# Fixing TensorE's order to that of the source in the pairs of a feed-forward block

## The chip, the cores and the metric

The kernel runs on one core of one Trainium2 chip. The metric is the device time of one execution in microseconds (us); lower is better. The core's engines run side by side, each with an instruction order of its own that is fixed when the program is compiled: TensorE (PE: matrix products; its weight loads are listed as PEld), VectorE (DVE), ScalarE (ACT), GpSimd (POOL) and SyncE (SP), which here issues almost all DMAs. An engine waits on semaphores for the others' results.

## The reference

Two layers of a decoder act on 256 tokens of width 2048, in float32. Of one layer:

```python
h = rms_norm(x, pre_mix_gain[i])
m = hybrid_mixer(h, ..., w_in[i], ..., w_out[i])    # attention and a gated recurrence
x = x + rms_norm(m, post_mix_gain[i])
h = rms_norm(x, pre_ffn_gain[i])
f = (silu(h @ w_ffn_gate[i]) * (h @ w_ffn_up[i])) @ w_ffn_down[i]    # 2048 -> 5632 -> 2048
x = x + rms_norm(f, post_ffn_gain[i])
gate = sigmoid(rms_norm(x, ple_gain[i]) @ w_ple_gate[i])
x = x + (p[i] @ w_ple_proj[i]) * gate
```

What matters here is the line of `f`: the gate, up and down products, with weights of 2048x5632, 2048x5632 and 5632x2048.

## The kernel before

**Precision.** Every float32 product is made of three products of the reduced type fp32r. A weight block of 128x1024 (two row blocks of 128, 512 columns) is fetched raw (`wr`, 10 buffers), ScalarE casts its high part (`wh`, 7 buffers, L305), VectorE subtracts to get the low part (`wl`, 7 buffers, L315), and activations have a high and a low part too. For each row block TensorE then issues high x high (L419), low x high (L422) and high x low (L423); a block thus takes six products, each 128x128 by 128x512. The order of the three is in `acc`, L415.

**Strips and pairs.** A strip computes one set of 512 output columns for both halves of the tokens (t = 0, 1). A pair (`paired`, L400) computes two sets of columns at once, into four PSUM banks. In a pair, a group of two blocks of rows, two sets of columns and two token halves is multiplied by the scheme of Strassen and Winograd: seven block products in place of eight, from sums of activations (`mixed`, `mixed_turned`) and differences of raw weights that VectorE makes in place (L435). The bank `u` carries product 1, is copied to SBUF by ScalarE (`saved`, L428), goes on with product 5 (`second`, L469), is copied again, goes on with product 7 (`third`, L473) and is copied once more; then it serves as the fourth output bank. The rest of the rows goes through `plain` (L483) as ordinary blocks, the first set of columns with the banks `acce` and `acca`, then the second set with `accc` and `u` (which is `ms` in the trace, as it comes from the pool of L107).

In source order a pair issues: products 1 (`u`), 2 (`accc`), 3 (`acce`), 4 (`acca`); the first plain block (`acce`, `acca`); product 5 (`u`); the further plain blocks of the first columns; product 6 (`accc`) and 7 (`u`); the plain blocks of the second columns. With `mixed_order` the last two plain blocks of both sets of columns come at the very end.

**The pairs of a layer.** The output projection has two pairs (L1144). The feed-forward block has ten pairs of a gate and an up column set (n = 1 to 10, `gated`, L1156; n = 0 goes as two strips), each with two sets of seven products (`more`), so 84 products in `fast` and 96 in `plain`. Between them stand the down products, in four groups of 2, 3, 3 and 3 column sets of hidden activations: each group makes a pair of output columns (0, 1) and a pair (2, 3), but the last group does (2, 3) as strips: seven down pairs, each with one set of seven. The per-layer gate at the end has one pair (L1283), with `after`.

**From the hidden block to the down pair.** `done_up` multiplies gate and up, transposes within blocks on VectorE (L251), stores to DRAM and fetches back in another order (`shuffled`, L241; SyncE issues both), and `split_shuffled` (L279) makes the high part on ScalarE (L203) and the low part on VectorE (L204). So the last hidden block of a group is still under way when the first down pair of that group starts. The transposed block, the fetched block, `saved` copies and gate values share the 12 buffers of the tag `nat` (L59).

**The order of the work.** The kernel is written against a scheduler that runs when the program is compiled. For each engine it takes, of the instructions whose inputs and buffers its own time model says are ready, the one that is earliest in the source; a later one may overtake an earlier one that it holds not to be ready. That order is then fixed; on the chip an engine takes its instructions strictly in it. `behind(...)` (L80) puts the instructions of a block, on the engine of a marked instruction, after that instruction.

Of the kernel before, what the change touches and what calls it, by code (L numbers as in the profile page):

```python
# [26 lines left out]
SKEW = 5  # L27
# [20 lines left out]
def decoder(ctx: ExitStack, tc: tile.TileContext, x, p, positions, w_in, attn_sinks,  # L48
# [16 lines left out]
    V, S, G, T = nc.vector, nc.scalar, nc.gpsimd, nc.tensor  # L65
# [13 lines left out]
    @contextmanager  # L79
    def behind(*names):  # L80

        with ExitStack() as st:
            for n in names:
                st.enter_context(tc.issue_after(marks[n].ins))
            yield
# [9 lines left out]
    def tick():  # L95
        clock[0] += 1
        for gen in list(running):
            if next(gen, True):
                running.remove(gen)
        for item in [q for q in queue if q[0] <= clock[0]]:  # L100
            queue.remove(item)
            item[1]()

    def nat(shape=(P, W), dt=F32):
        return np_.tile(list(shape), dt, tag="nat", name="nat")

    def bank(shape=(P, W)):  # L107
        return pms.tile(list(shape), F32, tag="ms", name="ms")
# [88 lines left out]
    def square_sum(src, acc, shape=(P, W)):  # L197
        j = np_.tile([P, W], F32, tag="junk", name="junk", bufs=1)
        S.activation(j[:, 0:shape[1]], src, AF.Square, accum_out=acc)
# [97 lines left out]
    def fetch_w(w, c, col):  # L297
        raw = wpr.tile([P, 2, W], F32, tag="wr", name="wr")
        nc.sync.dma_start(raw, w[c * 2 * P:(c + 1) * 2 * P, col:col + W].rearrange(
            "(k p) n -> p k n", p=P))  # L300
        return raw
# [6 lines left out]
    def load_w(w, c, col, raw=None, hi=None):  # L308

        if raw is None:  # L310
            raw = fetch_w(w, c, col)
        if hi is None:
            hi = high(raw)
        lo = wps.tile([P, 2, W], F32R, tag="wl", name="wl")
        marks["lo"] = V.tensor_tensor(lo, raw, hi.bitcast(F32), op=ALU.subtract)  # L315
        return hi, lo
# [81 lines left out]
        return both  # L398

    def paired(lhs, sums, wa, wb, cols, done_a, done_b, nch=8, row0=0, skews=(0, 0),  # L400
               after=None, mixed_order=False, more=None, q=0):

        base = row0 // (2 * P)
        opened = {}

        def psum(name):
            return pacc.tile([P, W], F32, tag="acc", name=name)

        def block(c, t):
            def get(k):  # L410
                kt = 2 * c + k
                return tuple(a[:, kt % 4, t * P:(t + 1) * P] for a in lhs[kt // 4])
            return get

        def acc(ps, x, hl, ks=(0, 1)):  # L415
            hi, lo = hl
            for k in ks:
                xh, xl = x(k)
                T.matmul(ps, xh, hi[:, k], start=id(ps) not in opened, stop=False,  # L419
                         skip_group_check=True)  # L420
                opened[id(ps)] = ps
                T.matmul(ps, xl, hi[:, k], start=False, stop=False, skip_group_check=True)  # L422
                marks["pe"] = T.matmul(ps, xh, lo[:, k], start=False, stop=k == ks[-1],  # L423
                                       skip_group_check=True)

        def saved(ps):
            b = nat()
            S.copy(b, ps)  # L428
            return b

        def parts(r):
            return load_w(None, 0, 0, raw=r)

        def sub(dst, p, q):
            V.tensor_tensor(dst, p, q, op=ALU.subtract)  # L435

        def fast():
            quads = [(sums(), q)] + ([(more(), q + 2)] if more else [])
            raw = [[fetch_w(w, base + c, col) for w, col in zip((wa, wb), cols)] for _, c in quads]
            for r, (_, c) in zip(raw, quads):  # L440
                r += [fetch_w(w, base + c + 1, col) for w, col in zip((wa, wb), cols)]

            def each(fn):
                for (mix, c), r in zip(quads, raw):
                    fn(mix, c, *r)
            u = psum("accu") if after else bank()
            each(lambda mix, c, r11, r12, r21, r22: acc(u, block(c, 0), parts(r11)))
            x = [saved(u)]
            each(lambda mix, c, r11, r12, r21, r22: sub(r11, r12, r11))
            cc = psum("accc")  # L450
            each(lambda mix, c, r11, r12, r21, r22: acc(cc, mix(1), parts(r11)))
            p5 = saved(cc)
            tick()
            e = psum("acce")
            each(lambda mix, c, r11, r12, r21, r22: acc(e, block(c + 1, 0), parts(r21)))
            if more:
                tick()

            def fourth(mix, c, r11, r12, r21, r22):
                sub(r11, r22, r11)  # L460
                sub(r21, r21, r11)
            each(fourth)
            a = psum("acca")
            each(lambda mix, c, r11, r12, r21, r22: acc(a, block(c + 1, 1), parts(r21)))
            tick()
            each(lambda mix, c, r11, r12, r21, r22: sub(r12, r22, r12))
            y = []

            def second():  # L469
                each(lambda mix, c, r11, r12, r21, r22: acc(u, mix(2), parts(r11)))  # L470
                y.append(saved(u))

            def third():  # L473
                each(lambda mix, c, r11, r12, r21, r22: acc(cc, mix(4), parts(r22)))
                each(lambda mix, c, r11, r12, r21, r22: acc(u, mix(3), parts(r12)))
                x.append(saved(u))
                y.append(p5)
                tick()
            return e, a, cc, u, x, y, second, third

        rest = [i for i in range(nch) if not q <= i < q + (4 if more else 2)]

        def plain(w, col, banks, skew, end, cs=rest, then=None):  # L483
            n = len(cs)
            ws = {}
            for i in range(n + skew):
                if i < n:
                    ws[i] = load_w(w, base + cs[i], col)
                    acc(banks[0], block(cs[i], 0), ws[i])
                    if i == n - 1 and end:  # L490
                        end(0)
                if i >= skew:
                    acc(banks[1], block(cs[i - skew], 1), ws[i - skew])
                if then and i == 0:
                    then()
                tick()
            if end:
                end(1)

        e, a, c, d, x1, x2, second, third = fast()  # L500

        def end_a(t):
            done_a(t, (e, a)[t], x1[t])

        def end_b(t):
            done_b(t, (c, d)[t], x2[t])
        if mixed_order:
            plain(wa, cols[0], (e, a), 0, None, cs=rest[:-2], then=second)
            third()
            plain(wb, cols[1], (c, d), 0, None, cs=rest[:-2])  # L510
            plain(wa, cols[0], (e, a), 0, end_a, cs=rest[-2:])
            plain(wb, cols[1], (c, d), 0, end_b, cs=rest[-2:])
            return
        def then():
            second()
            if after:
                after[0]()
        plain(wa, cols[0], (e, a), skews[0], lambda t: t or end_a(t), then=then)
        third()
        end_a(1)  # L520
        if after:
            after[1]()
        plain(wb, cols[1], (c, d), skews[1], end_b)

    def load_gain(g, col):
        b = np_.tile([P, W], F32, tag="gB", name="gB", bufs=2)
        nc.sync.dma_start(b, g[col:col + W].partition_broadcast(P))
        return b
# [199 lines left out]
    for l in range(DEPTH):  # L728
# [403 lines left out]
        def merged(s):  # L1132
            gB = load_gain(post_mix_gain[l], s * W)

            def done(t, ps):
                if t == 0:
                    mg.append(sp.tile([P, NT, W], F32, tag="ABCD"[s], name=f"mg{s}"))
                square_sum(ps, ssm[t][:, s:s + 1])
                V.tensor_tensor(mg[s][:, t], ps, gB, op=ALU.mult)
                if s == 3:  # L1140
                    post_norm(mg, ssm, t, ss, xT, gain_cols(32, l, 16), 4)
            return summed(done)
        for s in (0, 2):
            paired(mixT, lambda: sums, w_out[l], w_out[l], (s * W, s * W + W), merged(s),  # L1144
                   merged(s + 1), skews=(0, SKEW if s == 2 else 0))


        rx2 = lazy_rstd(ss, "ry")
# [41 lines left out]
        for gi, glen in enumerate(FF_GROUPS):  # L1190
# [11 lines left out]
            for s in range(4):  # L1202
# [31 lines left out]
                elif s % 2:  # L1234
                    paired(hid, lambda: hx[0], w_ffn_down[l], w_ffn_down[l], (s * W - W, s * W),
                           dones[s - 1], done, nch=2 * glen, row0=ff0 * W,
                           mixed_order=s == 1 and glen > 2, q=2)
# [37 lines left out]
        for s in (0, 1):  # L1275
# [3 lines left out]
            if s == 0:  # L1279
# [5 lines left out]
               after=(lambda: projected(2, pa), lambda: projected(3, pb)))  # L1285
# [32 lines left out]
```

## Time and profile before

| | |
|---|---|
| time, median of 3 runs (lowest to highest) | 2384.71 us (2380.53 to 2385.95) |
| the profiled execution, its own time | 2386.15 us |
| its span, first to last instruction | 2384.4 us |
| PE busy | 2351.7 us (99%), 10891 products |
| DVE busy | 2072.3 us (87%) |
| ACT busy | 1421.3 us (60%) |
| granted TensorE clock, mean | 0.997 |
| feed-forward pairs, first layer | 439.3 to 1060.3 us |
| feed-forward pairs, second layer | 1623.4 to 2244.1 us |

A row of the timeline gives the start, the length, the engine, the source line, the operation and `out<-in` by the program's names, and in brackets the engine's idle time before it with what ended it. A product has a length of some 0.39 us from its start to its modelled end, but products overlap in the array. A row of the windows gives, for a stretch, its length, and for each engine the busy time with the number of instructions, then the granted TensorE clock (1.00 is full), the share of the DMA engines' time and GB/s.

### The profile page before, as it was taken

The numbers are of one execution on the slowest core, as the hardware profiler recorded it, in microseconds if no ns is written. First come the engines' busy times: TensorE is split into PE (matmuls) and PEld (weight loads), VectorE is DVE, ScalarE is ACT, GpSimd is POOL, SyncE is SP. The second block draws the span as 40 slices with busy tenths as digits, with TensorE's granted clock in tenths as the row PEclk, the third lists the DMA queues.
The fourth block names the chain that finished last, engine by engine and source line by source line (L and its number), as shares of the span: only waits on it lengthen the run. The fifth ranks groups of instructions, "written<-read, shape, count | busy, mean of one in ns | idle before, by whom it ended". The sixth has DMA issues, their size and how long they took to land.

```text
span 2384.4 us, 31615 instructions
## 1 busy us (share of the span) xinstructions
PE 2351.7 (99%) x10891; PEld 1939.8 (81%) x10891; DVE 2072.3 (87%) x2671; ACT 1421.3 (60%) x2022; POOL 104.2 (4%) x213
## 2 busy tenths in 40 slices
PE   9999999999999999999999999999999999999999
PEld 7888887887888878888788888878777888888887
DVE  7687977999999999987877879779999999999885
ACT  6565466666656655656656554575666566566564
POOL 3100001000000000001010000010000000000010
PEclk9999999999999999999999999999999999999999
DMA  8666467666565764775766563774766576657853
GB/s 289 216 187 202 150 202 246 213 211 229 186 222 205 254 230 155 257 256 192 240 217 213 180 211 131 230 250 172 243 212 204 185 251 212 225 190 248 276 165 133
DMA packets 301666, 506.03 MB, mean 212 GB/s; under 512 B 23713, under 2 KB 69697, under 8 KB 301505
## 3 DMA queue, kind: packets, MB, share of 16 engines
q1 hardware_dynamic: 301200, 503.93, 63.2%
q8 instruction: 85, 1.39, 0.2%
q14 instruction: 77, 0.62, 0.1%
q0 software_dynamic: 64, 0.02, 0.0%
q10 hardware_dynamic: 240, 0.07, 0.0%
HBM read 474.57 MB, written 29.36 MB: 211 GB/s over the span
## 4 chain that ended last, share of the span: by engine, by line
PE 82%; DVE 11%; issue 3%; DMA 2%; ACT 1%; POOL 1%; SPq 0%; DVEq 0%; ACTq 0%; POOLq 0%
PE acc L330 9%; PE acc L331 9%; PE acc L333 9%; PE ms L419 5%; PE ms L423 5%; PE ms L422 5%; PE accc L423 4%; PE accc L422 4%; PE accc L419 4%; PE acca L423 4%; PE acca L419 4%; PE acca L422 4%; DVE wl L315 3%; PE acce L423 3%; PE acce L419 3%; PE acce L422 3%
## 5 line engine op out<-in xcount | busy, mean ns | idle before, releaser
L305 ACT CAST wh<-wr 128x1024 fp32r<-128x1024 f32 x1020 | 1039.0, 1052 | 699.6 <-DVE wr L435 222.2
L315 DVE TENSOR_TENSOR wl<-wr,wh 128x1024 fp32r<-128x1024 f32 x1020 | 1209.7, 1220 | 178.5 <-ACT wh L305 174.1
L330 PE MATMUL acc<-wh,ck 128*128 128x512 f32 x1056 | 418.0, 396 | 0.7 <-ACT ck L203 0.7
L331 PE MATMUL acc<-wh,ck 128*128 128x512 f32 x1056 | 413.2, 392 | 0.0
L333 PE MATMUL acc<-wl,ck 128*128 128x512 f32 x1056 | 411.8, 391 | 0.8 <-DVE wl L315 0.8
L435 DVE TENSOR_TENSOR wr<-wr 128x1024 f32<-128x1024 f32 x240 | 285.4, 1217 | 1.1
L333 PEld LDWEIGHTS acc<-wl,ck 128*128 128x128 f32 x1056 | 198.4, 188 | 42.8 <-DVE wl L315 1.7
L330 PEld LDWEIGHTS acc<-wh,ck 128*128 128x128 f32 x1056 | 198.8, 188 | 40.7 <-ACT ck L203 1.0
L331 PEld LDWEIGHTS acc<-wh,ck 128*128 128x128 f32 x1056 | 199.0, 188 | 39.9 <-DVE ck L204 0.2
L423 PE MATMUL acca<-wl,ck 128*128 128x512 f32 x448 | 177.3, 396 | 6.0 <-DVE wl L315 5.8
L419 PE MATMUL acca<-wh,ck 128*128 128x512 f32 x448 | 176.2, 393 | 2.3 <-ACT wh L305 1.6
L422 PE MATMUL acce<-wh,ck 128*128 128x512 f32 x448 | 175.0, 391 | 2.9 <-DVE ck L204 2.7
L419 PE MATMUL acce<-wh,ck 128*128 128x512 f32 x448 | 174.9, 390 | 2.7 <-ACT wh L305 2.7
L422 PE MATMUL acca<-wh,ck 128*128 128x512 f32 x448 | 175.6, 392 | 0.0
L423 PE MATMUL acce<-wl,ck 128*128 128x512 f32 x448 | 174.4, 389 | 0.0
L419 PE MATMUL ms<-wh,ck 128*128 128x512 f32 x420 | 164.7, 392 | 2.1 <-ACT nat L428 2.1
L422 PE MATMUL ms<-wh,ck 128*128 128x512 f32 x420 | 163.5, 389 | 0.0
L423 PE MATMUL ms<-wl,ck 128*128 128x512 f32 x420 | 163.2, 389 | 0.0
L422 PE MATMUL accc<-wh,ck 128*128 128x512 f32 x328 | 127.6, 389 | 0.0
L423 PE MATMUL accc<-wl,ck 128*128 128x512 f32 x328 | 127.6, 389 | 0.0
L419 PE MATMUL accc<-wh,ck 128*128 128x512 f32 x328 | 127.6, 389 | 0.0
L423 PEld LDWEIGHTS acca<-wl,ck 128*128 128x128 f32 x448 | 84.8, 189 | 29.5 <-DVE wl L315 11.5
(281 smaller groups left out, 3302.9 us busy)
## 6 DMA issues: line engine op xcount, KB each, us to landing
wr<-in_w_in_dram SPq DMA_DIRECT2D x176, 512.0 KB, 4.8
wr<-in_w_ffn_gate_dram SPq DMA_DIRECT2D x176, 512.0 KB, 5.5
wr<-in_w_ffn_up_dram SPq DMA_DIRECT2D x176, 512.0 KB, 6.2
wr<-in_w_ffn_down_dram SPq DMA_DIRECT2D x176, 512.0 KB, 7.1
wr<-in_w_out_dram SPq DMA_DIRECT2D x64, 512.0 KB, 4.8
wr<-in_w_ple_gate_dram SPq DMA_DIRECT2D x64, 512.0 KB, 5.3
turn<-nat SPq DMA_DIRECT2D x86, 256.0 KB, 2.1
nat<-turn SPq DMA_DIRECT2D x344, 64.0 KB, 3.4
```

Source lines behind the costliest of these rows:

```text
L305: marks["hi"] = S.copy(hi, raw)
L315: marks["lo"] = V.tensor_tensor(lo, raw, hi.bitcast(F32), op=ALU.subtract)
L330: T.matmul(ps[t], xh, hi[:, k], start=first, stop=False)
L331: T.matmul(ps[t], xl, hi[:, k], start=False, stop=False)
L333: marks[t, c] = marks["pe"] = T.matmul(ps[t], xh, lo[:, k], start=False, stop=last)
L419: T.matmul(ps, xh, hi[:, k], start=id(ps) not in opened, stop=False, skip_group_check=True)
L422: T.matmul(ps, xl, hi[:, k], start=False, stop=False, skip_group_check=True)
L423: marks["pe"] = T.matmul(ps, xh, lo[:, k], start=False, stop=k == ks[-1], skip_group_check=True)
L435: V.tensor_tensor(dst, p, q, op=ALU.subtract)
```

## The change

All TensorE instructions that `paired` issues are put under a manual schedule of that one engine, so that TensorE keeps the order of the source within a pair. The products of `fast` (1 to 4, and what it defines) are moreover put behind the last product issued before in the source (`behind("pe")`), so that a pair does not start before the one ahead of it has ended. Pairs with `after` (the per-layer gate) and pairs called with the new argument `free=True` (the output projection) keep the scheduler's order. So the 10 gate and up pairs and the 7 down pairs of each layer are concerned. The body of `paired` moves into an inner function `products`, with nothing else changed. No instruction is added or removed on any engine, no tile, buffer or DMA changes.

```diff
     def paired(lhs, sums, wa, wb, cols, done_a, done_b, nch=8, row0=0, skews=(0, 0),
-               after=None, mixed_order=False, more=None, q=0):
+               after=None, mixed_order=False, more=None, q=0, free=False):
...
-        e, a, c, d, x1, x2, second, third = fast()
+
+        def products(pin):
+            with behind("pe") if pin else nullcontext():
+                e, a, c, d, x1, x2, second, third = fast()
...
+            if mixed_order:
+                plain(wa, cols[0], (e, a), 0, None, cs=rest[:-2], then=second)
+                third()
+                plain(wb, cols[1], (c, d), 0, None, cs=rest[:-2])
+                plain(wa, cols[0], (e, a), 0, end_a, cs=rest[-2:])
+                plain(wb, cols[1], (c, d), 0, end_b, cs=rest[-2:])
+                return
...
+            plain(wa, cols[0], (e, a), skews[0], lambda t: t or end_a(t), then=then)
             third()
...
+            plain(wb, cols[1], (c, d), skews[1], end_b)
+
+        pin = not (after or free)
+        with tc.manual_schedule(engines={T.engine}) if pin else nullcontext():
+            products(pin)
...
             paired(mixT, lambda: sums, w_out[l], w_out[l], (s * W, s * W + W), merged(s),
-                   merged(s + 1), skews=(0, SKEW if s == 2 else 0))
+                   merged(s + 1), skews=(0, SKEW if s == 2 else 0), free=True)
```

More of the change, by code (lines that the diff above doesn't have):

```diff
@@ L498, in plain, with end_a, end_b, then @@
                 end(1)
-        e, a, c, d, x1, x2, second, third = fast()
[L502 to L508, printed above, removed]
-            third()
[L510 to L515, printed above, removed]
-            if after:
[L517 to L523, printed above, removed]
+        def products(pin):
+            with behind("pe") if pin else nullcontext():
+                e, a, c, d, x1, x2, second, third = fast()
+            def end_a(t):
+                done_a(t, (e, a)[t], x1[t])
+            def end_b(t):
+                done_b(t, (c, d)[t], x2[t])
+            if mixed_order:
[5 more added lines that the diff above has]
+                return
+            def then():
+                second()
+                if after:
+                    after[0]()
+            plain(wa, cols[0], (e, a), skews[0], lambda t: t or end_a(t), then=then)
+            third()
+            end_a(1)
+            if after:
+                after[1]()
+            plain(wb, cols[1], (c, d), skews[1], end_b)
+        pin = not (after or free)
+        with tc.manual_schedule(engines={T.engine}) if pin else nullcontext():
+            products(pin)
     def load_gain(g, col):
```

## The prediction

> **What bounds the kernel now.** I read the first part of the page, then a table by stage (the feed-forward pairs of both layers), then the timelines of TensorE and ScalarE where TensorE's order differs from that of the source.
>
> ```profile
> span 2384.4 us, 31615 instructions
> ...
> PE 2351.7 (99%) x10891; PEld 1939.8 (81%) x10891; DVE 2072.3 (87%) x2671; ACT 1421.3 (60%) x2022; POOL 104.2 (4%) x213
> ```
>
> ```profile
> core 0: us, PE busy (x) PEld busy (x) DVE busy (x) ACT busy (x) POOL busy (x), PEclk, DMA share, GB/s
> 439.30:1060.30 621.00, 612.37 (x2676) 501.08 (x2674) 586.72 (x596) 381.19 (x439) 0.00 (x0) 1.00 0.65 222
> 1623.40:2244.10 620.70, 612.41 (x2676) 501.23 (x2674) 586.65 (x596) 381.18 (x439) 0.00 (x0) 1.00 0.65 222
> ```
>
> TensorE is the bound, and the two stages that the change touches last 621 us each. With products that start every 0.227 us (below: 658.06 to 658.28), the 2670 products of the ten gate and up pairs (180 each) and seven down pairs (two of 90, five of 138) need 2670 x 0.2268 = 605.5 us. So some 15 us of each stage, 30 in all, is all that a better order of products could win. VectorE is close behind (587 of 621), so where TensorE waits, it is often for VectorE.
>
> **Where the order differs.** I laid the banks in TensorE's timeline against the order of the source. Ten of the seventeen pairs of a layer have it already; the change does nothing there. Seven differ, alike in both layers: gate and up pairs n = 1, 2, 3, in which two products of the first plain block overtake the end of product 4, and the first down pair of each of the four groups, in which the whole second plain block overtakes product 5. In the second group's:
>
> ```profile
> 658.06 0.39 PE L423 MATMUL acca<-wl,ck 128*128 128x512 f32 x1
> 658.28 0.39 PE L419 MATMUL acce<-wh,ck 128*128 128x512 f32 x1
> ...
> 662.56 0.50 PE L419 MATMUL ms<-wh,nat 128*128 128x512 f32 x1 [0.52 <-ACT nat L428]
> ```
>
> The `ms<-wh,nat` of 662.56 is product 5; in the source it stands at 658.28. It waits for ScalarE's copy (L428) of product 1 out of the same bank. This is ScalarE there, and SyncE's fetch of the group's last hidden half:
>
> ```profile
> 658.25 1.06 ACT L305 CAST wh<-wr 128x1024 fp32r<-128x1024 f32 x1 [1.34 <-PE acca L422]
> 659.22 0.61 ACT L203 CAST ck<-nat 128x512 fp32r<-128x512 f32 x1
> 660.98 1.05 ACT L305 CAST wh<-wr 128x1024 fp32r<-128x1024 f32 x1 [1.15 <-PE acca L422]
> 661.93 0.58 ACT L428 COPY nat<-ms 128x512 f32<-128x512 f32 x1
> ```
>
> ```profile
> 659.61 1.75 SPq L264 DMA_DIRECT2D nat<-turn  x4
> ```
>
> The copy stands in ScalarE's order behind the split of the hidden block (L203) and one more weight cast. The fetch and the copy both take a `nat` buffer, and the fetch is earlier in the source; I read the late copy as the scheduler handing these buffers out in source order. The fetch's own date depends on the end of the pair before, not on the order inside this one, so I expect the copy to stay late.
>
> **The change part by part.** No engine gets an instruction more or less, and no DMA moves by the edit itself. What it costs or saves is waits.
>
> *Product 5 in its place, last three groups.* The cast of 660.98 waits for TensorE to free a weight buffer, which the overtaking block does; in the new order that block is behind product 5, so this cast must come after the copy. The copy is then next behind the split: 659.22 + 0.61 + 0.53 (the copy's 0.58, as these overlap by 0.05 to 0.09), so product 5 starts at about 660.4, a wait of 2.1 us from 658.28. Behind it wait twelve products whose operands are there and, for the buffer, the cast of 660.98 with the low part that VectorE makes from it. Before, 14 products (3.18 us) filled the 4.28 us to 662.56, so 1.10 was lost. The other first down pairs:
>
> ```profile
> 529.52 0.39 PE L419 MATMUL acce<-wh,ck 128*128 128x512 f32 x1
> ...
> 539.81 0.50 PE L419 MATMUL ms<-wh,ck 128*128 128x512 f32 x1 [1.07 <-ACT nat L428]
> ...
> 846.86 0.39 PE L419 MATMUL acce<-wh,ck 128*128 128x512 f32 x1
> ...
> 2219.26 0.39 PE L419 MATMUL acce<-wh,ck 128*128 128x512 f32 x1
> ...
> 2223.54 0.50 PE L419 MATMUL ms<-wh,nat 128*128 128x512 f32 x1 [0.49 <-ACT nat L428]
> ```
>
> ```profile
> 531.00 0.62 ACT L203 CAST ck<-nat 128x512 fp32r<-128x512 f32 x1 [0.46 <-DMA nat<-turn]
> ...
> 848.33 0.62 ACT L203 CAST ck<-nat 128x512 fp32r<-128x512 f32 x1 [0.44 <-DMA nat<-turn]
> ...
> 2220.90 0.62 ACT L203 CAST ck<-nat 128x512 fp32r<-128x512 f32 x1 [0.61 <-DMA nat<-turn]
> ```
>
> By the same steps the wait is 848.33 + 1.2 - 846.86 = 2.7 and, for the last of the six, 2220.90 + 1.2 - 2219.26 = 2.85. The other three lie near the first. Four of 2.13 with these two make 14.1, 2.35 on average, in place of six losses of about 1.15 (2219.26 to 2223.54 is again 4.28 with 14 products): **+7.2 us**. Bounds for one wait: nothing, if the copy leaves as soon as product 1 is done; 4.28, if it stays at its old time. I take the split's end, the nearest row that nothing in the change moves.
>
> *Product 5 in the first group.* The wait is 531.00 + 1.2 - 529.52 = 2.65, in place of 1.2 lost at 539.81: 1.4 us late in the first layer, about as much in the second. I cost it at nothing, because TensorE runs into VectorE right after:
>
> ```profile
> 520.00:574.00 54.00, 51.51 (x225) 41.71 (x223) 52.80 (x55) 33.11 (x40) 0.00 (x0) 1.00 0.53 176
> ```
>
> ```profile
> 573.63 3.49 DVE L315 TENSOR_TENSOR wl<-wr,wh 128x1024 fp32r<-128x1024 f32 x3
> ```
>
> VectorE is busy 52.8 of 54 us until the low part for product 4 of pair n = 3 (573.63 + 1.22 = 574.85), and TensorE, done with product 3 at 571.7, has two products to do until then. Without this cover it is 2 x 1.4 = 2.8 us.
>
> *The clock at n = 3.* That wait has a second price:
>
> ```profile
> 571.80:575.20 3.40, 1.26 (x5) 0.74 (x5) 3.40 (x4) 3.31 (x4) 0.00 (x0) 1.00 0.00 0
> 575.30:578.70 3.40, 3.40 (x10) 2.62 (x9) 3.40 (x4) 2.41 (x4) 0.00 (x0) 0.50 0.72 227
> 848.30:851.70 3.40, 2.28 (x11) 1.57 (x10) 3.40 (x4) 2.64 (x4) 0.00 (x0) 1.00 0.93 288
> ```
>
> After 3.4 us with only 1.26 busy the granted clock is 0.50 for 3.4 us, which costs half of it, 1.7 us. After 2.28 busy in 3.4 it stays at 1.00. If TensorE arrives at n = 3 over a microsecond later, its idle time there falls to about one and this loss goes, in both layers: **-3.4**. But the six new waits leave 3.4 - 2.35 = 1.05 us busy if one lies whole in such a stretch. A wait that is split between two stretches leaves both busier. I take half of them: 3 x 1.7 = **+5.1** (bounds 0 and 10.2).
>
> The Trainium skill ("TensorE: Matmul & The Clock Gate", section "HAM oscillation — how this bites in real kernels") has another limit: "The abstract rule is "no PE-idle gaps >~3.4µs."" No gap here comes near that, yet the rows show the clock at 0.50, so the measurement decides; by the page alone the 5.1 would be nothing, which is the first rival below.
>
> *The two products at n = 1 and n = 2.*
>
> ```profile
> 489.57 3.50 DVE L315 TENSOR_TENSOR wl<-wr,wh 128x1024 fp32r<-128x1024 f32 x3
> ```
>
> ```profile
> 490.14 0.39 PE L419 MATMUL acce<-wh,ck 128*128 128x512 f32 x1
> 490.36 0.39 PE L422 MATMUL acce<-wh,ck 128*128 128x512 f32 x1
> 490.85 0.50 PE L423 MATMUL acca<-wl,ck 128*128 128x512 f32 x1
> ```
>
> At n = 2 product 4 needs the first low part of the VectorE row (489.57 + 1.22 = 490.79) and goes on at 490.85 in any case; the two products (0.45 us) that were done meanwhile come later. I take as much at n = 1. Nothing gives these back: 4 x 0.45 = **+1.8** for both layers.
>
> **Sum**: 7.2 - 3.4 + 5.1 + 1.8 = +10.7 us on the profiled execution's 2386.15 (a span of 2384.4 and 1.75 around it): 2396.8. That execution is 1.4 above the median of 2384.71, so **2395 us**, +0.4%.
>
> **The rivals.**
>
> *The clock holds (2390).* The new waits are single ones and may fall across two stretches. Then 10.7 - 5.1 = +5.6: 2391.8, or 2390 against the median. For it: 848.30 to 851.70, with a gap of over a microsecond, kept its clock. Against it: 1.05 busy is less than the 1.26 that lost it.
>
> *The waits are given back (2388).* While TensorE stands, VectorE may get ahead and shorten TensorE's later waits for low parts:
>
> ```profile
> L423 PE MATMUL acca<-wl,ck 128*128 128x512 f32 x448 | 177.3, 396 | 6.0 <-DVE wl L315 5.8
> ```
>
> All of these, 6.0 and about 0.16 of hidden gap on each of eleven, are 7.8 us: 10.7 - 7.8 = +2.9, 2388. Against it: VectorE's low parts need ScalarE's casts, and the cast at 658.25 waits for TensorE to free one of seven buffers, so neither can run far ahead.
>
> *The copies leave in time (2374, faster).* If, with TensorE's order fixed, the scheduler puts the copy of product 1 ahead of the split, product 5 never waits. Place: the eight first down pairs; price: the 6 x 1.15 and 2 x 1.2 lost there come back, with the 3.4 at n = 3, less the 1.8: -10.9, 2374. It decides once the copy ends before TensorE reaches product 5 (658.28). For it: ScalarE is idle 1.34 us ahead of 658.25. Against it: the fetch of 659.61 is not moved by the change.
>
> *The copies stay at their old time (2412).* A wait of 4.28 six times: 6 x 3.13 = 18.8, every one with the clock, 10.2, then -3.4 + 1.8: +27.4.
>
> *It does nothing (2385).* The order may be kept as a mere preference; the ten pairs that have it show that the scheduler mostly follows it anyway.
>
> **How the numbers follow.** Forecast 0.42 (its own range 2390 to 2402: none to six stretches at half the clock, and two more for the waits), clock holds 0.15, given back 0.13, copies in time 0.17, copies late 0.08, nothing 0.05. A measurement of this kernel can tell about 0.2%, 4.8 us, from no change. Slower by more (over 2389.5): nearly all of the forecast, over half of the clock's case, a fifth of the giving back and the late copies, 0.59. Faster by more: the copies in time and a little, 0.18. Within: 0.23. The range runs from 2377 to 2408; it leaves out most of the case of early copies and most of that of late ones, under 0.2 together.
>
> **What would show it.** In the first down pair of each group, product 5 right behind the first plain block, with an idle time of about 2.1 to 2.9 us that ends on ScalarE's copy, and the copy right behind a split (L203); the next 3.4 us at a clock of 0.50 in some of them; n = 3 without the clock at 0.50; at n = 1 and 2 product 4 whole, ahead of the first plain block; the ten other pairs as before. It is wrong if product 5 finds its copy done, if the order of the casts on ScalarE or of the differences on VectorE changes in pairs that had the source's order, or if the waits for low parts shrink.

## The result and the profile after

The changed kernel takes **2400.94 us** (median of 4 runs, 2400.4 to 2403.78), the kernel before beside it 2385.24: the ratio of the means is 1.0072, 95% interval 1.0055 to 1.009, so it is 0.7% slower. The forecast was 2395, slower. The profiled execution's span is 2399.7 us, 15.3 more than before.

The page's head, and the two stages in the table of windows (columns as before):

```profile
span 2399.7 us, 31647 instructions
...
PE 2355.8 (98%) x10891; PEld 1944.9 (81%) x10891; DVE 2075.7 (86%) x2671; ACT 1423.2 (59%) x2022; POOL 104.4 (4%) x213
```

```profile
437.50:1065.70 628.20, 614.35 (x2676) 503.84 (x2675) 590.85 (x599) 382.96 (x440) 0.00 (x0) 0.99 0.65 221
1629.00:2259.40 630.40, 615.29 (x2676) 504.45 (x2674) 590.94 (x599) 382.13 (x440) 0.00 (x0) 0.99 0.65 220
```

The stages last 628.2 and 630.4 us, where they lasted 621.0 and 620.7: 7.2 and 9.7 more, 16.9 together. The rest of the kernel, which the change does not touch, is 1.6 shorter. Most of this is one stretch of 3.4 us at half the clock near the start, which this execution did not have (first row before, second after):

```profile
8.70:12.10 3.40, 3.37 (x8) 2.65 (x9) 3.40 (x5) 2.93 (x6) 1.40 (x33) 0.50 0.90 301
```

```profile
8.70:12.10 3.40, 3.37 (x18) 2.69 (x18) 3.22 (x5) 2.52 (x6) 1.41 (x33) 1.00 0.94 313
```

The number of products is the same; the loss in the stages is waits and, behind them, the clock. One group of products shows the waits, the first row from before, the second from after:

```profile
L419 PE MATMUL ms<-wh,nat 128*128 128x512 f32 x56 | 22.9, 408 | 1.6 <-ACT nat L428 1.6
```

```profile
L419 PE MATMUL ms<-wh,nat 128*128 128x512 f32 x56 | 25.3, 451 | 20.5 <-ACT nat L428 20.5
```

Product 5 of the down pairs (it is in the group `ms<-wh,nat`) waits 20.5 us in all for ScalarE's copy, where it waited 1.6. These are eight waits, one in the first down pair of each group. A gap hides another 0.16 us (a product lasts 0.39 us to its modelled end, but the next one can start after 0.23), so the eight cost 21.8. The place that the prediction showed, in the second group of the first layer, first TensorE, then ScalarE:

```profile
656.15 0.39 PE L423 MATMUL acca<-wl,ck 128*128 128x512 f32 x1
658.61 0.50 PE L419 MATMUL ms<-wh,nat 128*128 128x512 f32 x1 [2.07 <-ACT nat L428]
```

```profile
656.35 1.04 ACT L305 CAST wh<-wr 128x1024 fp32r<-128x1024 f32 x1 [0.77 <-PE acca L422]
657.45 0.62 ACT L203 CAST ck<-nat 128x512 fp32r<-128x512 f32 x1
657.97 0.58 ACT L428 COPY nat<-ms 128x512 f32<-128x512 f32 x1
658.45 0.59 ACT L428 COPY nat<-accc 128x512 f32<-128x512 f32 x1
660.07 1.05 ACT L305 CAST wh<-wr 128x1024 fp32r<-128x1024 f32 x1 [1.03 <-PE ms L422]
```

Product 5 now follows the first plain block, and the copy follows the split. The next cast has moved behind the copy, since its buffer is freed by product 5 (`ms L422`). And this is what follows four of the waits, in the table of windows:

```profile
528.40:531.80 3.40, 0.50 (x3) 0.23 (x2) 3.40 (x5) 2.43 (x4) 0.00 (x0) 1.00 0.97 321
531.90:535.30 3.40, 3.40 (x9) 2.65 (x8) 3.35 (x3) 0.11 (x1) 0.00 (x0) 0.50 0.76 188
654.70:658.10 3.40, 1.83 (x9) 1.18 (x7) 3.40 (x4) 2.57 (x4) 0.00 (x0) 1.00 0.92 257
658.20:661.60 3.40, 3.00 (x13) 2.48 (x14) 3.40 (x5) 2.37 (x4) 0.00 (x0) 1.00 0.92 307
...
1036.90:1040.40 3.50, 1.63 (x8) 1.02 (x6) 3.50 (x4) 2.16 (x5) 0.00 (x0) 1.00 1.07 288
1040.50:1043.90 3.40, 3.40 (x8) 2.72 (x9) 3.35 (x4) 1.30 (x2) 0.00 (x0) 0.50 0.98 287
2228.10:2231.50 3.40, 1.37 (x7) 0.79 (x5) 3.40 (x4) 1.98 (x2) 0.00 (x0) 1.00 0.75 212
2231.70:2235.10 3.40, 1.79 (x4) 1.49 (x5) 3.33 (x4) 1.59 (x3) 0.00 (x0) 0.51 0.96 299
```

Six of the eight waits are followed by the clock at half, one of them for two stretches (from 2231.7 on): seven stretches of 3.4 us in the two stages, where there were two before. The two that are not are those of the second groups, as the one at 656 to 659 us, which lies in two stretches.

From the timelines, the time from the last product of the pair ahead to the last of the pair, in us, layer 1 and layer 2 (n = 1 counts from its own first product; the other pairs differ by 0.5 at most):

| pairs | before | after | difference |
|---|---|---|---|
| n = 1 and 2 | 81.8, 81.9 | 82.6, 82.6 | +0.8, +0.7 |
| first group's two down pairs and n = 3 | 87.3, 87.3 | 86.4, 86.5 | -0.9, -0.8 |
| second group's first down pair | 32.8, 32.8 | 35.0, 34.2 | +2.2, +1.4 |
| third group's first down pair | 33.8, 32.8 | 36.3, 35.5 | +2.5, +2.7 |
| last group's first down pair | 32.6, 32.6 | 35.1, 37.9 | +2.5, +5.3 |

### The profile page after: what moved, and what is told of

Read it like the earlier page. It is cut to its first block, busy times and chain, and to the rows that moved or that the text cites. A ratio compares the mean times of both kernels' runs of the same rounds, so it can differ in the third digit from the quotient of the medians.

```text
span 2399.7 us, 31647 instructions
## 1 busy us (share of the span) xinstructions
PE 2355.8 (98%) x10891; PEld 1944.9 (81%) x10891; DVE 2075.7 (86%) x2671; ACT 1423.2 (59%) x2022; POOL 104.4 (4%) x213
## 4 chain that ended last, share of the span: by engine, by line
PE 81%; DVE 12%; issue 2%; DMA 2%; ACT 1%; POOL 1%; SPq 1%; DVEq 0%; ACTq 0%; POOLq 0%
PE acc L331 9%; PE acc L333 9%; PE acc L330 9%; PE ms L419 5%; PE ms L423 4%; PE ms L422 4%; PE acca L423 4%; PE accc L422 4%; PE accc L419 4%; PE accc L423 4%; DVE wr L435 4%; PE acca L419 4%; PE acca L422 4%; DVE wl L315 4%; PE acce L419 3%; PE acce L422 3%
## 5 line engine op out<-in xcount | busy, mean ns | idle before, releaser
L422 PE MATMUL acce<-wh,ck 128*128 128x512 f32 x448 | 175.7, 392 | 0.0
L422 PE MATMUL acca<-wh,ck 128*128 128x512 f32 x448 | 174.5, 390 | 0.0
L422 PE MATMUL ms<-wh,ck 128*128 128x512 f32 x420 | 163.5, 389 | 0.0
L422 PE MATMUL accc<-wh,ck 128*128 128x512 f32 x328 | 127.6, 389 | 0.0
```

## The experiments

Theory A: product 5 of the first down pair of a group waits because ScalarE's copy of product 1 comes late, and it comes late because the scheduler hands out the `nat` buffers in the order of the source, behind the fetch of the last hidden half. The waits cost their length, and the clock at half behind them costs again. The rivals are in the expectations: that the fixed order costs by itself (B), that the clock at half costs nothing of its own (C), that no `nat` buffer is free (D), that ScalarE's split or casts hold the copy (E).

**The copy of product 1 in a buffer of its own, order fixed (own).**

```diff
-            b = nat()
+            b = np_.tile([P, W], F32, tag="junk", name="one", bufs=1) if own else nat()
...
-            x = [saved(u)]
+            x = [saved(u, own)]
...
-                           mixed_order=s == 1 and glen > 2, q=2)
+                           mixed_order=s == 1 and glen > 2, q=2, own=s == 1)
```

> The changed kernel, but in the first down pair of each group the copy of product 1 goes to a buffer of its own (the one of the tag junk, idle there) and no longer takes one of the 12 nat buffers. Nothing is left out. Theory A (the loss is the wait of product 5 for a copy that ScalarE makes late because the nat buffers are handed out in source order): the eight waits of product 5 (21.8 us in the changed kernel) and the seven stretches at half the clock (11 us) go, TensorE is early at pair n = 3 again and waits there for VectorE as before (8 us with its clock): 2401 - 33 + 8 = 2376, faster than before. Rival B (the fixed order itself costs, by what it does to the orders of ScalarE and VectorE): the copy is early, and the time stays near 2395 to 2401.

Measured: 2376.21 us (2374.32 to 2378.73), 0.9968 of before (0.9957 to 0.9979): faster than both kernels. ScalarE, TensorE there, and the group of product 5:

```profile
648.64 1.99 ACT L305 CAST wh<-wr 128x1024 fp32r<-128x1024 f32 x2
650.54 0.57 ACT L428 COPY one<-ms 128x512 f32<-128x512 f32 x1
651.01 4.85 ACT L305 CAST wh<-wr 128x1024 fp32r<-128x1024 f32 x5
```

```profile
655.97 0.39 PE L423 MATMUL acca<-wl,ck 128*128 128x512 f32 x1
656.19 0.39 PE L419 MATMUL ms<-wh,nat 128*128 128x512 f32 x1
```

```profile
L419 PE MATMUL ms<-wh,nat 128*128 128x512 f32 x56 | 21.8, 389 | 0.0
```

The copy is made between the casts, eight microseconds ahead of the split, and product 5 follows the plain block without a gap. The clock never drops in the stages (1.000 on average). The order is still that of the source, so B falls: the fixed order itself does not cost the 16 us.

**The same buffer without the fixed order (own_free).** The edit of own, in the kernel before.

> The kernel before, in the scheduler's order, with the same buffer for the copy of product 1. Nothing is left out. Theory A: with the copy in time the scheduler sees no reason to let the second plain block overtake product 5, so TensorE's order is nearly that of the source without being fixed, and the time is that of the fixed order with the same buffer to within 4 us (about 2376). Rival B: without the fixed order it is faster by 10 us or more than with it.

Measured: 2375.63 us (2374.99 to 2376.46), 0.9965 of before (0.9953 to 0.9978), within 0.6 us of own. Once the copy is in time, it does not matter whether the order is fixed or left to the scheduler.

**Product 5 behind the second plain block (five_late).**

```diff
-                if then and i == 0:
+                if then and i == five:
...
-                           mixed_order=s == 1 and glen > 2, q=2)
+                           mixed_order=s == 1 and glen > 2, q=2, five=s == 1)
```

> The changed kernel with product 5 written after the second plain block in the first down pair of each group, so TensorE's order is again fixed but has the overtaking in it. Nothing is left out. Theory A: 2.72 us of products fill the waits, which fall from 2.1 to 3.1 to 0 to 0.4 (the one of 4.0 to 1.3); the clock stays at full speed there, pair n = 3 waits for VectorE again: 2401 - 20 - 11 + 8 = 2378. Rival B: fixing the order costs by itself, 2395 to 2401.

Measured: 2390.86 us (2389.64 to 2395.3), 1.0031 of before (1.002 to 1.0042): 10 us better than the changed kernel, not the 23 of A. ScalarE and TensorE in the second group, and the products that wait for copies:

```profile
659.46 0.62 ACT L203 CAST ck<-nat 128x512 fp32r<-128x512 f32 x1 [0.23 <-DMA nat<-turn]
660.90 1.04 ACT L305 CAST wh<-wr 128x1024 fp32r<-128x1024 f32 x1 [0.81 <-PE acca L422]
661.85 0.58 ACT L428 COPY nat<-ms 128x512 f32<-128x512 f32 x1
```

```profile
660.70 0.39 PE L423 MATMUL acca<-wl,ck 128*128 128x512 f32 x1
662.48 0.50 PE L419 MATMUL ms<-wh,nat 128*128 128x512 f32 x1 [1.39 <-ACT nat L428]
```

```profile
L419 PE MATMUL ms<-wh,nat 128*128 128x512 f32 x56 | 23.4, 418 | 9.2 <-ACT nat L428 9.0
L419 PE MATMUL ms<-wh,ck 128*128 128x512 f32 x420 | 164.9, 393 | 5.7 <-ACT nat L428 5.7
```

The number of A forgot the cast: with the second plain block ahead of product 5, the cast of 660.90 has its buffer again and stands ahead of the copy, as it did before the change. So the wait is 1.4 in six places, where A had 0 to 0.4 in five of them. The second row is the wait for product 7's copy, 5.7 us against 2.1 before: there the scheduler's order had put products of later blocks in the gap. One stretch of the stages is at half the clock (540.2 us, behind such a wait). So there is some truth in B: where the copies are late, fixing this order costs some 7 us over the scheduler's, which fills such gaps with whatever is ready; 1.6 of the 7 are at n = 1 and 2.

**Products that nobody reads in the wait (fill).**

```diff
             def second():
+                if fill:
+                    idle = bank((P, 2, SEQ))
+                    for _ in range(fill):
+                        T.matmul(idle, block(q, 0)(0)[0], lhs[q // 2][0][:, 0:2],
+                                 start=True, stop=True)
```

> The changed kernel with eight products ahead of product 5 in the first down pair of each group whose result nobody reads (128x128 by 128x512, 1.8 us in all); nothing of the computation is left out. Theory A: they fit into the waits of 2.1 to 4.0 us, which end when they ended, but the idle time falls to 0.3 to 1.3 (one of 2.2), so the clock stays at full speed in six or seven of the seven stretches: 6 to 7 times 1.6, less some 3 that come back as TensorE's waiting at n = 3: 2392 to 2395. Rival C (the halved clock is a sign and costs nothing of its own, as TensorE waits for VectorE after it anyway): 2401, or more by the products added.

Measured: 2394.52 us (2391.81 to 2396.29), 1.004 of before (1.0027 to 1.0054). The same place, TensorE and the clock around two of the waits:

```profile
657.95 1.98 PE L473 MATMUL ms<-ck 128*128 128x512 f32 x8
660.25 0.50 PE L419 MATMUL ms<-wh,nat 128*128 128x512 f32 x1 [0.32 <-ACT nat L428]
```

```profile
532.00:535.40 3.40, 2.29 (x10) 1.57 (x10) 3.40 (x5) 1.76 (x4) 0.00 (x0) 1.00 0.87 277
535.40:538.80 3.40, 3.40 (x17) 2.82 (x16) 3.33 (x4) 1.69 (x3) 0.00 (x0) 1.00 0.82 203
```

With 64 products more the kernel is 6.4 us faster than the changed one. The waits end as they did, at the copy; none of the stages' stretches is at half the clock (the next 3.4 us hold 17 products where 9 stood). So the clock's loss is one of its own, and C falls.

**One `nat` buffer more (spare).** In the last gate and up pair of a group the copy of product 5 leaves `nat`.

```diff
-                y.append(saved(u))
+                y.append(saved(u, own))
...
-                   summed(done_up), more=lambda: sx[1])
+                   summed(done_up), more=lambda: sx[1], own=last)
```

> The changed kernel; in the last gate and up pair of each group the copy of product 5 goes to the buffer of the tag junk instead of one of the 12 nat buffers, so that from there to the end of that pair one nat buffer more is free. Nothing is left out. Theory A1 (the copy of product 1 stands late because nat buffers are handed out in source order, behind the fetch of the last hidden half): nothing changes, 2398 to 2403, product 5 waits 2 to 4 us in eight places. Rival D (there is no free nat buffer then): the copy comes earlier, the waits of product 5 shrink to under 1 us, 2376 to 2388.

Measured: 2401.11 us (2397.69 to 2406.16), 1.0078 of before (1.0064 to 1.0091), as the changed kernel. Product 5 waits as long as there:

```profile
L419 PE MATMUL ms<-wh,nat 128*128 128x512 f32 x56 | 24.1, 430 | 21.4 <-ACT nat L428 21.4
```

A buffer more in that pair does not help. It is one more only to the end of that pair, so this run alone does not exclude D for the time of the copy. A count does: by the source and the timeline of the changed kernel, at most seven of the twelve `nat` buffers hold something between 651 and 658 us, at the second group of the first layer (four sums for the down pair, and of the last hidden block a gate value and its transposed and fetched halves). A buffer is free all that time, so D falls.

**The last fetch out of `nat` (last_fetch).** The buffer goes to the fetch instead; the copy stays in `nat`.

```diff
-            d = nat((P, n * P))
+            d = np_.tile([P, W], F32, tag="junk", name="got", bufs=1) if own else nat((P, n * P))
...
-                d = shuffled(gate[t], slow=False)
+                d = shuffled(gate[t], slow=False, own=last and t == 1)
```

> The changed kernel; the fetch of the last hidden half of each group (token half 1 of the last gate and up pair) lands in the buffer of the tag junk instead of a nat buffer. The copy of product 1 stays in nat. Nothing is left out. Theory A1 (source order): the copy now has to come only after the transposition of that half, some 4 us earlier on ScalarE, ahead of the split; product 5 waits nowhere, 2376 to 2380. Rival E (the copy is held by the split or the casts on ScalarE and not by the fetch's buffer): as the changed kernel, 2398 to 2403.

Measured: 2376.98 us (2375.19 to 2378.28), 0.9972 of before (0.9961 to 0.9982), as own. ScalarE:

```profile
655.65 0.57 ACT L428 COPY nat<-ms 128x512 f32<-128x512 f32 x1
656.13 0.58 ACT L428 COPY nat<-accc 128x512 f32<-128x512 f32 x1
656.60 2.19 ACT L305 CAST wh<-wr 128x1024 fp32r<-128x1024 f32 x2
658.70 0.61 ACT L203 CAST ck<-nat 128x512 fp32r<-128x512 f32 x1
```

The fetch, earlier in the source, no longer asks for a buffer of the same tag, and the copy moved ahead of the split. It now starts 0.45 us after the transposition of that half on VectorE (L251, 654.50 to 655.20), which is the request for a `nat` buffer that stands next ahead of it in the source. With the count of free buffers this shows that the copy was held by its place in the line for `nat` buffers and not by their number; E falls.

**The order of the source in one kind of pair alone (gates, downs).** `free=True` in the call of the other kind.

> The order of the source in the gate and up pairs alone; the down pairs keep the scheduler's order. Nothing is left out. Theory A: only products 4 of pairs n = 1, 2, 3 change; 0.4 us each at n = 1 and 2 in both layers, nothing at n = 3, where the clock still halves: 2384 + 1.6 = 2385 to 2387, no difference that can be told. Rival B: a good part of the 16 us is here, 2390 or more.

> The order of the source in the down pairs alone; the gate and up pairs keep the scheduler's order. Nothing is left out. Theory A: the whole loss but for 1.6 us is here: 2397 to 2401, with product 5's waits of 2 to 4 us. Rival B: 2390 or less.

Measured: gates 2387.13 us (2384.24 to 2391.59), 1.0016 of before (1.0007 to 1.0025); downs 2396.67 us (2395.69 to 2396.77), 1.0056 (1.0041 to 1.0071). Nearly all of the loss is in the down pairs; both figures are a little off A's, upward by some 2 us in gates and just below its range in downs. In the profile of gates the clock is at half in one stretch of the stages (not at n = 3, where A had it, but in the first down pair of layer 2), in that of downs in three, against seven of the changed kernel. A few microseconds between such runs are this count, and so are those between executions of one kernel: the eleven of gates took 2384.2 to 2385.0 us at a mean granted clock of 0.999 or 1.000, 2385.5 to 2389.3 at 0.998, and 2390.1 and 2391.6 at 0.997.

## Why the prediction was right, point by point

*Which pairs change.* Right: seven of the seventeen pairs of a layer, and the ten others last as long as before to within 0.5 us.

*The copy stays late, right behind the split.* Right, and for the reason given: own, last_fetch and the count of free buffers show that it is the line for `nat` buffers. The rival "copies in time" (2374) did not happen with this change, but own came near its number, 2376, by making it true.

*Six sites, a wait of 14.1.* Measured 15.6: 2.2, 3.0 and 2.1 in the first layer, 2.1, 2.2 and 4.0 in the second, each with the hidden 0.16. The four that were taken as 2.13 are right; the one of 2.7 came to 3.0, and the one of 2.85 to 4.0, as the hidden half comes later there:

```profile
2232.16 0.62 ACT L203 CAST ck<-nat 128x512 fp32r<-128x512 f32 x1 [1.83 <-DMA nat<-turn]
2232.68 0.58 ACT L428 COPY nat<-ms 128x512 f32<-128x512 f32 x1
```

ScalarE stood 1.83 us for that fetch, where it stood 0.61 before. What sends the fetch later stays open.

*The first group, costed at nothing.* The cover was there: product 4 of n = 3 no longer waits at all. (In the profile before, its two gaps there end on ScalarE's casts, 0.79 and 1.35 us, and not on VectorE; the first of these casts had waited 1.79 us for VectorE.) But the term "-3.4" for the clock at n = 3 was **mis-sized**. The first group's own waits, 3.1 us in both layers, bring the clock to half at product 5, and the prediction counted the clock behind the other six alone. So this loss did not go, it moved from n = 3 to the first down pair: that pair takes 3.4 and 3.5 us more, n = 3 takes 4.3 less. By the table the stretch gains 0.9 and 0.8, not 1.7 and 1.7.

*The clock behind the six waits, three stretches, +5.1.* **Mis-sized** too: four of the six waits and one of them twice, five stretches. The six sites cost 2.2 + 1.4 + 2.5 + 2.7 + 2.5 + 5.3 = 16.6 in all, where 7.2 + 5.1 = 12.3 was forecast. These 4.3 and the 1.7 at n = 3 are nearly all of the 6.2 us between the forecast's 10.7 and the stages' 16.9. The prediction halved the six for waits that are split between two stretches. That happened to the two of 2.2 and 2.1 us in the second groups. A wait of 3 us is rarely split so that neither part counts (one of 3.0 in spare was, into 1.0 and 1.8), and the one of 4 is followed by two stretches. That four of six counted and not three was chance as far as is known; that one can count twice was overlooked.

*n = 1 and 2, +1.8.* Measured 1.5, and right in kind: at n = 2 product 4 now waits 0.43 us for its low part, the gap that the two products had filled.

*The rivals.* The clock did not hold. The waits were not given back: product 4's waits for low parts are

```profile
L423 PE MATMUL acca<-wl,ck 128*128 128x512 f32 x448 | 176.0, 393 | 7.1 <-DVE wl L315 6.8
```

against 6.0, so TensorE's waits for VectorE did not shrink. The forecast's sum, 10.7 on the execution's own time, met 15.3, so the size was a third short, and without the 1.6 that came back near the start by chance it would have been shorter still. The range, 2377 to 2408, was wide enough to hold a small gain as well; it is the places and the lengths of the waits that speak for the prediction, and not the range.

## What to carry to other kernels

An order that the scheduler made up may look like noise and be the cover of a wait; before fixing it, look at what the overtaken instruction was waiting for, and remove that. Here the cause was a copy that shared a tag of buffers with a fetch that is earlier in the source but ready later, and a buffer of its own for the copy is worth 0.3% against before in either order (0.9968 and 0.9965). Count a TensorE wait of two microseconds or more with the slow stretch that may follow it.

## What the runs showed of the hardware

The price of a wait was larger than its length, since the granted clock may be halved behind it. In each of the ten traces the changes of the clock lie whole multiples of 3.413 us apart: in the changed kernel the stretches at half begin at 531.90, 849.34 and 1040.48 us and so on, and these are 93 and 56 times 3.413 us apart. Counted on this grid, in the two stages of all ten traces, 20 stretches at full clock had 1.9 us or more idle, and 18 of them were followed by one at half the clock. With less than 1.7 us idle none was. In between two were (1.77 and 1.79 us) and two were not (1.78 and 1.81). So it depends on where a wait falls on the grid whether it costs the clock. In own a wait of 1.53 us at n = 3 of the second layer, whole in one stretch, left the clock at full speed:

```profile
1750.15:1753.56 3.41, 1.88 (x8) 1.08 (x8) 3.41 (x4) 3.33 (x5) 0.00 (x0) 1.00 0.00 0
1753.56:1756.97 3.41, 3.02 (x14) 2.18 (x13) 3.41 (x4) 2.40 (x3) 0.00 (x0) 1.00 0.81 252
```

So where a stretch is idle for about half of its time the next one is at risk, and eight products of no use in each of the eight waits of two to four microseconds made the whole kernel 6.4 us faster.
